# Two parts of a modulation vector summed on TensorE instead of VectorE, with a new order of steps, in a two-layer trunk on one core

## The chip, the core and the metric

The kernel runs on one core of one Trainium2 chip. The metric is the device time of one execution in microseconds (us), lower is better. The engines are named as the profile names them: PE is TensorE (its matmuls; PEld its weight loads, which run beside them), DVE is VectorE, ACT is ScalarE, POOL is GpSimd, SP is SyncE, which issues most DMAs.

## What is computed

A trunk of two layers over 512 positions with 1024 features each. Around every layer stands a modulation that depends on one vector c alone:

```python
cond = jax.nn.silu(c)
for l in range(DEPTH):                       # DEPTH = 2
    mod = cond @ ada_w[l] + ada_b[l]         # ada_w[l] is 1024 x 3072
    shift, scale, gate = jnp.split(mod, 3, axis=-1)
    h = rms_norm(x, norm_g[l]) * (1.0 + scale[:, None, :]) + shift[:, None, :]
    ...                                      # layer 0: conv + RWKV-7 heads, layer 1: sparse attention
    x = x + gate * mixed
```

The change touches `cond @ ada_w[l]`: a vector of 1024 times a matrix. Shift and scale of layer 0 are computed at the kernel's start, and gate of layer 1 near its end (both of these already on PE). What stays, gate of layer 0, shift of layer 1 and scale of layer 1, is 3 x 1024 numbers, in six parts of 512: the later modulation, M0 to M5.

Layer 0 has two halves that share one projection: a convolution of width 31 followed by a layer norm and two gates, and 16 RWKV-7 heads, done in eight pairs (a pair is called a head below, 0 to 7), each a recurrence over 8 chunks of 64 positions. Both go through one output projection. Layer 1 is attention over 16 heads with an indexer that keeps 128 keys for each query.

## The kernel before

**Layout and precision.** Features lie on the 128 partitions, the 512 positions along the free dimension. All dense products split both operands into a high and a low half and take three products per 128 x 128 weight tile (L369). For that, ACT writes a weight tile's high half (L355), and the low half is a subtraction on DVE or POOL (`low`, L337 to L339), chosen by step: steps named in the table `LOWV` use DVE.

**What sets the order.** The table `ORDER` lists layer 0 as steps: D (dense k, r, v of a head), P (prep), O (operands of the recurrence), G (gate), V (a conv block), A (the conv branch's gate), S (a triangular solve: 31 pairs of steps on DVE, L585 to L591, and DMA round trips), T (its second half on PE: 32x32 matmuls, L611 to L626), C (the chain over 8 chunks, L628 to L674), N (norm of a head, with a transpose `pyT` at L689), M0 to M5 (the later modulation), ln (layer norm statistics), Y and Z (the two halves' results), E (a1: output projection of 7 of the heads plus the conv branch's first part, `zo8qN`), W and F (a2: the rest of the output projection, `zo0qN`). A scheduler emits the steps in this order into the five engines' queues, shifted by priorities: the table `PRIO` gives an offset for a step or a tile ("0S" the solve's tiles, "pvar" the sums of the layer norm's variance, "1K" layer 1's keys, and so on). Each engine then runs its own queue in order and waits for others by semaphores. `START` and `ORDER1` do the same for the first steps and for layer 1.

**The chain, one chunk.** Two products `px` from the state SV; a copy to X on ACT (L649); two more `px`; two `py` and, after a copy of SV on ACT (L662), `py<-SV,BKn`, which carries the state on; then DVE adds it to the decayed state: `SV<-py,sw` (L671). The next chunk's first product waits for that addition. Each float32 matmul stands twice in the trace's counts (x4 there is 2 in the code).

**A part of the later modulation, `ada_col(n)`, L726 to L745.** Eight tiles `at` of 128 x 512 are loaded on ACT's DMA queue (L732); DVE multiplies the first by a column of `cond` (L734) and adds the other seven in turn into `ac` (L736: 128 x 512 each); then four one-column matmuls with a column of ones sum over the partitions (`pmc`, L740, a 128 x 128 weight load each), and DVE adds the bias into `modc` (L742). From the step `late` on, `at` and `ac` come from a pool with 4 buffers that `yb`, `xa`, `xl` and `sq` (tiles of Y, E and F) share.

**Layer norm.** ln sums the squares of eight blocks `yc` on POOL (`vs`, L866); four one-column matmuls `pvar` (L870), a root taken over DVE and POOL (`rs`, L209 and L210), a copy (L200) and a transpose-broadcast `pbc` (L203) follow; the Z steps wait for the result.

Of the kernel before, what the change touches and what calls it, by code (L numbers as in the profile page):

```python
# [10 lines left out]
F32 = mybir.dt.float32  # L11
F32R = mybir.dt.float32r
I32 = mybir.dt.int32
AF = mybir.ActivationFunctionType
# [4 lines left out]
P = 128  # L19
D = 1024  # L20
S = 512
KT = D // P
# [14 lines left out]


ORDER = """
D0 lora V0 P0 D1 D2 O0 G0 P1 P2 O1 S0.1 T0 C0 V1 T1 C1 M0 rot D3 O2 P3 M1 O3 N0 G1 D4 G2 S2.3 V3 A6 T2 C2 P4 V4 D5  # L40
T3 V2 O4 N2 P5 A7 C3 G3 O5 S4.5 V6 N1 G4 T4 C4 V5 N3 M4 T5 V7 C5 D6 A2 P6 G5 O6 D7 P7 O7 A1 S6 G7 T6 late G6 N4 A3
A0 Y3 A4 Y4 N5 S7 A5 ln M3 C6 Y0 Z7 T7 N6 Y1 C7 Z3 Y2 M2 Y5 Z6 Y6 Z0 E6 E3 Z1 E1 M5 E4 Z2 E2 E5 E0 N7 E7 Z5 Z4 W
F7.1 F5 F1 F7.0 F4 F0 F2 F3 F6.0 F6.1
"""


PRIO = {"conv": -1552, "0D": -465, "0N": 74, "1K": -464, "1w": -326, "1x": -48, "0S": 206, "0M": -31, "1y": -15, "0rot": 1, "0G": -123, "1m": -706, "0lora": 36, "0A": -118, "1I": 556, "0Y": -189, "0Z": 12, "pmean": 97, "0V": 5, "0late": 493, "pvar": -495, "pbn": -87, "1k": -9, "xs": 74}


LOWV = ('0A', '0D', '0E', '0F', '0G', '0N', '0V', '0Y', '0Z', '1e', '1ki', '1qi', '1v', '1y')  # L50


ACT0 = "XBrt"


START = """
x0 b0 a0 g1 g2 h0 g3 b1 h1 a1 b2 z0.3 z0.1 z0.0 x4 x5 a2 h3 a3 h2 x6 z0.2 h5 h4 x7 z2.2 z1.2 z1.1 z1.0 z2.3 z1.3 b3
z2.1 h6 z2.0 h7 z3.0 z3.2 z3.1 z3.3
"""


# [12 lines left out]
def trunk(ctx: ExitStack, tc: tile.TileContext, x, c, positions, ada_w, ada_b, norm_g, final_g,  # L74
# [3 lines left out]
    V, A, G, T, DQ = nc.vector, nc.scalar, nc.gpsimd, nc.tensor, nc.sync  # L78
# [5 lines left out]

    PR = PRIO

    def prio(key):
        return tc.high_priority(offset=PR[key]) if key in PR else nullcontext()
# [5 lines left out]
    cst = ctx.enter_context(tc.tile_pool(name="cst", bufs=1))  # L94
# [5 lines left out]
    def zps(name="z"):  # L100
        return ps.tile([P, 512], F32, tag="z", bufs=3, name=name)

    def tps(tag, bufs):
        return lambda shape, name: ps.tile(shape, F32, tag=tag, bufs=bufs, name=name)


    cps, pps, aps = tps("c", 2), tps("p", 2), tps("a", 1)


    ident = cst.tile([P, P], F32, name="ident")  # L110
# [27 lines left out]
    ones_col = ones_m[:, 0:1]  # L138
# [7 lines left out]
    for tb in range(TB):  # L146
        t = pa.tile([P, D], F32, tag="x", bufs=5, name="xt")
# [20 lines left out]
    nc.scalar.dma_start(prm3, bass.AP(tensor=conv_w.tensor, offset=conv_w.offset,  # L168
                                      ap=[[P, 124], [124 * P, 2], [1, P]]))

    cond = cst.tile([P, KT], F32, name="cond")
    tc_ = cst.tile([P, KT], F32, name="tc_")
    A.activation(tc_, cc, AF.Tanh, scale=0.5)
    V.scalar_tensor_tensor(out=cond, in0=tc_, scalar=1.0, in1=cc, op0=OP.add, op1=OP.mult)
# [4 lines left out]
    C0 = (C_LORA, C_K, C_R, C_V)  # L179
    at0, w0 = [[None, None] for _ in range(4)], []  # L180
    for w in "w0 00 w1 11 01 w2 10 21 20 31 w3 30".split():
        i, n = w[0], int(w[1])
# [63 lines left out]
    Z0 = [zps("z0") for _ in range(3)] + [cps([P, 512], "z0") for _ in range(4 - 3)]  # L246
# [67 lines left out]
    S0 = dict(a=lambda q: mod0(q, 0), b=lambda q: mod0(q, 1), x=lambda k: xn(k, "D"), g=lambda k: xn(k, "G"), h=h0, z=z0)  # L314
# [77 lines left out]
    def slab(tag, bufs, name, dt=F32):  # L392
        return pq.tile([P, 512], dt, tag=tag, bufs=bufs, name=name)
# [332 lines left out]
    def ada_col(n, slab):  # L726

        l, c0 = (0, 2 * D + n * 512) if n < 2 else (1, (n - 2) * 512)
        ac = slab("ac")
        for k in range(KT):  # L730
            t = slab("at")
            nc.scalar.dma_start(t, ada_v[l, :, k, c0:c0 + 512])  # L732
            if k == 0:
                V.tensor_scalar(ac, t, cond[:, 0:1], None, op0=OP.mult)  # L734
            else:
                V.scalar_tensor_tensor(out=ac, in0=t, scalar=cond[:, k:k + 1], in1=ac, op0=OP.mult, op1=OP.add)  # L736
        pm = aps([P, 4], "pmc")
        for j in range(4):
            with prio("pm"):
                T.matmul(pm[:, j:j + 1], lhsT=ac[:, j * P:(j + 1) * P], rhs=ones_col, start=True, stop=True)  # L740
        m_ = modc[:, n * 4:n * 4 + 4]
        V.tensor_tensor(out=m_, in0=pm, in1=ab(l, (2, 0, 1)[n // 2])[:, n % 2 * 4:n % 2 * 4 + 4], op=OP.add)  # L742
        if n >= 4:
            V.scalar_tensor_tensor(out=m_, in0=m_, scalar=1.0, in1=PT2[:, 56 + (n - 4) * 4:60 + (n - 4) * 4],
                                   op0=OP.add, op1=OP.mult)  # L745
# [245 lines left out]
    def ops(h):  # L991
# [3 lines left out]
        lora=lora, rot=rotary, D=dense_h, P=lambda h: hp_prep(h, D_[h]), O=ops, S=lambda *h: hp_solve(h),  # L995
        T=lambda h: hp_solve2(H[h]), C=lambda h: hp_chain(H[h]), G=lambda h: hp_gate(h, H[h]),
# [36 lines left out]
    for tb in range(TB):  # L1033
        t = asl("pen", 4, "pen")
# [274 lines left out]
```

## Time and profile before

| | us |
|---|---|
| three runs before | 1263.14, 1264.27, 1270.81 |
| median | 1264.27 |
| the profiled execution | 1265.15 |
| its span in the trace | 1263.3 |
| PE busy in the span | 1169.2 (93%) |
| DVE / ACT / POOL busy | 983.0 (78%) / 610.1 (48%) / 311.4 (25%) |
| mean granted clock of PE | 0.946 of full speed |

The profile is that of one execution. Busy shares are averages over stages; the granted clock is 1.00 where PE runs at its upper level and 0.50 at its lower, and a stretch between is a mix of both. The rows that the prediction uses stand in the section below.

### The profile page before, as it was taken

To read this page: it belongs to the slowest core of one execution; us is meant where nothing else is said; L and a number is where in the kernel's file an instruction comes from. 1 tells how busy PE (TensorE), PEld (TensorE's weight loads), DVE (VectorE), ACT (ScalarE), POOL (GpSimd) and SP (SyncE) were. 2 spreads that over 40 slices of the span, in tenths; PEclk is the share of its full clock that TensorE was granted. 3 is DMA by queue.
4 is the path that set the end of the run, shared out by engine and by line. 5 is a ranking of instruction groups with operands and counts; after the bars stand their busy time and mean duration, and the time that the engine had idled before them with its cause. 6 is when DMAs were issued, how large, how long until landed. Compare 5 with 4: busy or idle time off the path is not lost. (4 is left out here: it accounts for less than half of the span.)

```text
span 1263.3 us, 19449 instructions
## 1 busy us (share of the span) xinstructions
PE 1169.2 (93%) x6984; PEld 930.0 (74%) x6984; DVE 983.0 (78%) x2080; ACT 610.1 (48%) x1322; POOL 311.4 (25%) x344
## 2 busy tenths in 40 slices
PE   5999999999999999989689998899999999999997
PEld 2676677878776777766568787776777788888886
DVE  5759888669878998887876646679999899958732
ACT  4355454653355444445345334445453566636433
POOL 3113113210223111421232003424565110020042
PEclk8899998899979998999578999899999999999998
DMA  9623335323311323125555743643444422232122
GB/s 291 181 68 99 88 103 159 105 73 109 83 56 55 105 65 92 52 71 165 169 169 184 216 146 100 197 105 117 125 134 125 138 64 75 56 100 62 49 86 84
DMA packets 204007, 142.83 MB, mean 113 GB/s; under 512 B 33373, under 2 KB 176134, under 8 KB 203910
## 3 DMA queue, kind: packets, MB, share of 16 engines
q1 hardware_dynamic: 187616, 114.88, 31.6%
q10 hardware_dynamic: 16294, 26.70, 7.3%
q8 instruction: 55, 0.90, 0.3%
q14 instruction: 42, 0.34, 0.1%
HBM read 117.69 MB, written 17.83 MB: 107 GB/s over the span
## 5 line engine op out<-in xcount | busy, mean ns | idle before, releaser
L355 ACT ACTIVATE wh<-st 128x512 fp32r<-128x512 f32 (+2 forms) x256 | 148.7, 606 | 211.1 <-issue 34.6
L339 POOL TENSOR_TENSOR wl<-st,wh 128x512 fp32r<-128x512 f32 x82 | 115.0, 1416 | 306.1 <-ACT wh L355 298.8
L713 DVE SCALAR_TENSOR_TENSOR cacc<-u,PT,cacc 128x512 f32<-128x512 f32 x240 | 183.3, 782 | 1.5
L339 DVE TENSOR_TENSOR wl<-st,wh 128x512 fp32r<-128x512 f32 (+2 forms) x174 | 115.4, 674 | 44.9 <-ACT wh L355 44.7
L659 POOL TENSOR_TENSOR sw<-SV,W 64x128 f32<-64x128 f32 x56 | 59.1, 1059 | 130.0 <-DVE SV L671 118.9
L1186 ACT ACTIVATE lm<-lm,mx 128x512 f32<-128x512 f32 x64 | 46.1, 720 | 32.4 <-DVE mx L1185 32.3
L1194 ACT ACTIVATE pth<-pt 128x512 fp32r<-128x512 f32 x64 | 37.7, 593 | 35.4 <-PE pt L1192 28.5
L1183 DVE CUSTOM_DVE_ANT_0 lm<-pl,pen 128x512 f32<-128x512 f32 x64 | 43.3, 682 | 10.9 <-PE pl L1177 8.2
L1195 DVE TENSOR_TENSOR ptl<-pt,pth 128x512 fp32r<-128x512 f32 x64 | 43.5, 685 | 5.9 <-ACT pth L1194 5.8
L673 ACT ACTIVATE Y<-py 64x128 f32<-64x128 f32 x64 | 17.1, 267 | 55.9 <-DVE SV L671 48.1
L1122 DVE MATCH_REPLACE8 sc<-m,sc 128x512 f32<-128x512 f32 x64 | 42.8, 675 | 0.0
L1192 PE MATMUL pt<-ident,lm 128*128 128x128 f32 x256 | 39.1, 275 | 3.8 <-DVE lm L1188 2.3
L589 DVE TENSOR_TENSOR tmp<-TA,En 128x126 f32<-128x126 f32 (+37 forms) x155 | 40.5, 261 | 2.1
L1121 DVE MAX8 m<-sc 128x8 f32<-128x512 f32 x64 | 41.4, 681 | 0.0
L640 PEld LDWEIGHTS px<-SV,LTR 128*65 128x65 f32 x256 | 26.4, 158 | 20.1 <-DVE SV L671 13.5
L591 DVE TENSOR_TENSOR En<-En,tmp 128x126 f32<-128x126 f32 (+37 forms) x155 | 38.7, 250 | 2.2
L640 PEld LDWEIGHTS py<-SV,BKn 128*65 128x65 f32 x224 | 21.1, 155 | 25.4 <-ACT SV L662 22.9
L1192 PEld LDWEIGHTS pt<-ident,lm 128*128 128x128 f32 x256 | 29.3, 140 | 13.0 <-issue 8.6
L736 DVE SCALAR_TENSOR_TENSOR ac<-at,cond,ac 128x512 f32<-128x512 f32 x42 | 32.9, 783 | 7.5 <-DMA at<-in_ada_w 7.5
L640 PE MATMUL px<-SV,LTR 128*65 128x64 f32 x256 | 30.5, 249 | 8.1 <-DVE SV L671 7.4
L1208 PE MATMUL pO<-pth,vrh 128*128 128x256 f32 x128 | 37.1, 290 | 0.6 <-DVE gr L1212 0.6
L662 ACT ACTIVATE SV<-px 64x128 f32<-64x128 f32 x64 | 17.2, 269 | 41.8 <-PE px L640 26.6
(1262 smaller groups left out, 3775.9 us busy)
## 6 DMA issues: line engine op xcount, KB each, us to landing
st<-in_even_w_in SPq DMA_DIRECT2D x57, 512.0 KB, 4.1
st<-in_odd_w_in SPq DMA_DIRECT2D x38, 512.0 KB, 4.6
at<-in_ada_w ACTq DMA_DIRECT2D x48, 256.0 KB, 2.7
ast<-in_ada_w SPq DMA_DIRECT2D x8, 1024.0 KB, 10.7
st<-in_odd_w_out SPq DMA_DIRECT2D x16, 512.0 KB, 4.0
st<-in_even_w_out SPq DMA_DIRECT2D x9, 512.0 KB, 4.2
yc<-cv_d SPq DMA_DIRECT2D x16, 256.0 KB, 3.9
gt<-in_ada_w ACTq DMA_DIRECT2D x16, 256.0 KB, 3.8
```

What stands on the lines that cost most here:

```text
L339: (V if STEP[0] in LOWV else G).tensor_tensor(out=dst, in0=src, in1=hi.bitcast(F32), op=OP.subtract)
L355: A.activation(wh[c_], st[c_], AF.Copy)
L589: V.tensor_tensor(out=tv, in0=TA[:, j, j + 1:32, None].to_broadcast([P, n, m]), in1=E_[:, j:j + 1, :m].to_broadcast([P, n, m]), op=OP.mult)
L640: T.matmul(out[0:m, s_], lhsT=L[r_, o:o + m], rhs=rhs[r_], skip_group_check=True, **k_)
L659: G.tensor_tensor(out=f2(sw), in0=f2(SV[0:64, c_]), in1=wb, op=OP.mult)
L713: V.scalar_tensor_tensor(out=ac, in0=u[:, j:j + S], scalar=wcol(j), in1=ac, op0=OP.mult, op1=OP.add)
L1121: V.max(out=m8, in_=sc)
L1122: V.match_replace(out=sc, in_to_replace=m8, in_values=sc, imm_value=-3e38)
L1183: V.tensor_tensor_reduce(out=lm, in0=pl, in1=pen[tb], scale=1.0, scalar=-3e38, op0=OP.add, op1=OP.max, accum_out=mx[:, 0:1])
L1186: A.activation(lm, lm, AF.Exp, scale=ISQ, bias=mx[:, 1:2], accum_out=mx[:, 2:3])
L1192: T.transpose(pt[:, sb], lm[:, sb * P:(sb + 1) * P], ident)
L1195: V.tensor_tensor(out=ptl[:, :, s2], in0=pt, in1=pth[:, :, s2].bitcast(F32), op=OP.subtract)
```

## The change

Parts M3 and M5 (`MPE = "35"`) are summed by matmuls: for each of the eight `at` tiles PE adds `condw[:, k:k+65]` (transposed) times the tile to a 65 x 512 sum `p_row`; the vector c's tile is widened by 64 columns of zeros so that 65 columns can be taken from any k. Row 0 of the sum is the wanted one. ACT copies it into `ac`, and the four one-column matmuls pick row 0 with a column of the identity in place of the ones. M0, M1, M2 and M4 stay on DVE. Besides, `ORDER` (layer 0), `START`, `PRIO` and `LOWV` have new values. `ORDER1`'s text is the same.

```diff
-PRIO = {"conv": -1552, "0D": -465, "0N": 74, "1K": -464, "1w": -326, ..., "0S": 206, ..., "0lora": 36, ..., "0late": 493, "pvar": -495, ..., "xs": 74}
+PRIO = {"conv": -1552, "0D": -465, "0N": 76, "1K": -490, "1w": 8, ..., "0S": 289, ..., "0lora": 76, ..., "0late": 1067, "pvar": -430, ..., "pyT": 8, "pt": -23, ...}
...
-LOWV = ('0A', '0D', '0E', '0F', '0G', '0N', '0V', '0Y', '0Z', '1e', '1ki', '1qi', '1v', '1y')
+LOWV = ('0A', '0D', '0E', '0F', '0G', '0N', '0V', '0Y', '0Z', '1e', '1f', '1ki', '1v', '1y')
+MPE = "35"
...
-    cond = cst.tile([P, KT], F32, name="cond")
+    condw = cst.tile([P, KT + 64], F32, name="condw")
+    G.memset(condw[:, KT:], 0.0)
+    cond = condw[:, 0:KT]
...
         ac = slab("ac")
+        pe = str(n) in MPE
+        p_row = aps([65, 512], "p_row1") if pe else None
         for k in range(KT):
             t = slab("at")
             nc.scalar.dma_start(t, ada_v[l, :, k, c0:c0 + 512])
-            if k == 0:
+            if pe:
+                T.matmul(p_row, lhsT=condw[:, k:k + 65], rhs=t, start=k == 0, stop=k == KT - 1)
+            elif k == 0:
                 V.tensor_scalar(ac, t, cond[:, 0:1], None, op0=OP.mult)
             else:
                 V.scalar_tensor_tensor(out=ac, in0=t, scalar=cond[:, k:k + 1], in1=ac, op0=OP.mult, op1=OP.add)
+        r_ = slice(0, 65 if pe else P)
+        if pe:
+            A.activation(ac[0:65], p_row, AF.Copy)
         pm = aps([P, 4], "pmc")
         for j in range(4):
             with prio("pm"):
-                T.matmul(pm[:, j:j + 1], lhsT=ac[:, j * P:(j + 1) * P], rhs=ones_col, start=True, stop=True)
+                T.matmul(pm[:, j:j + 1], lhsT=ac[r_, j * P:(j + 1) * P], rhs=ident[r_, 0:1] if pe else ones_col,
+                         start=True, stop=True)
```

Counted over the whole program, PE gets 16 matmuls `p_row` more; DVE has 14 multiply-adds and 2 multiplications of 128 x 512 fewer; ACT has 2 copies of 65 x 512 more; POOL has one memset more and 8 low halves fewer, DVE 8 low halves more (16 of layer 1's output projection come to it, 8 of the indexer's queries leave it). DMAs are the same in number and size. The line numbers after are larger by 6 to 14.

The order moves at many places of layer 0. Three of them matter below.

The first is PE's queue in the chain of head 6 (C6), where M3 stands. `px` and `py` are the chain's products, `pvar` and `pbc` belong to the layer norm. Before, with the chain's first chunk in the first two rows:

```order
L640 MATMUL py<-SV,BKn 65x64 x2
L640 MATMUL py<-SV,Q 65x64 x2
L870 MATMUL pvar<-ones_m,vs 128x1 x4
L640 MATMUL px<-SV,LTR 65x64 x2
L640 MATMUL py<-SV,LTR 65x64 x2
L203 MATMUL pbc<-ident,vs 128x128 x4
L640 MATMUL px<-X_544,Q 65x64 x2
L640 MATMUL py<-SV,BKn 65x64 x2
L640 MATMUL py<-SV,Q 65x64 x2
L640 MATMUL px<-SV,LTR 65x64 x2
```

After, from the end of the chain's second chunk:

```order
L884 MATMUL pvar<-ones_m,vs 128x1 x4
L742 MATMUL p_row_5955<-at,condw 65x512
L209 MATMUL pbc<-ident,vs 128x128 x4
L646 MATMUL px<-SV,LTR 65x64 x2
L742 MATMUL p_row_5955<-at,condw 65x512
L646 MATMUL py<-SV,LTR 65x64
L742 MATMUL p_row_5955<-at,condw 65x512
L646 MATMUL px<-X_544,Q 65x64 x2
L646 MATMUL py<-SV,LTR 65x64
L742 MATMUL p_row_5955<-at,condw 65x512
L646 MATMUL py<-SV,BKn 65x64 x2
L646 MATMUL py<-SV,Q 65x64 x2
```

Two chunks of the chain now stand ahead of `pvar`, where one stood, and the eight `p_row` are laid between the products of the third and fourth chunk. The eight `p_row` of M5 stand in E, after head 7's chain, between the products of `zo8q2x` and `zo8q4x`.

The second is DVE's queue at the same place. `rs<-pvar` needs `pvar` from PE; `SV<-py,sw` carries the chain from one chunk to the next; `tmp` and `En` are the solve of head 7 (S7). Before:

```order
L848 SCALAR_TENSOR_TENSOR yc<-yc,mean 128x512
L589 TENSOR_TENSOR tmp<-TA,En 128x68
L209 TENSOR_SCALAR rs_5943<-pvar 128x4
L591 TENSOR_TENSOR En<-En,tmp 128x17x4
L671 TENSOR_TENSOR SV<-py,sw 64x128
L589 TENSOR_TENSOR tmp<-TA,En 128x64
L200 COPY vs<-rs_5943 128x512
L591 TENSOR_TENSOR En<-En,tmp 128x16x4
```

After:

```order
L677 TENSOR_TENSOR SV<-py,sw 64x128
L595 TENSOR_TENSOR tmp<-TA,En 128x72
L862 SCALAR_TENSOR_TENSOR yc<-yc,mean 128x512
L597 TENSOR_TENSOR En<-En,tmp 128x18x4
L595 TENSOR_TENSOR tmp<-TA,En 128x68
L597 TENSOR_TENSOR En<-En,tmp 128x17x4
L862 SCALAR_TENSOR_TENSOR yc<-yc,mean 128x512
L595 TENSOR_TENSOR tmp<-TA,En 128x64
L597 TENSOR_TENSOR En<-En,tmp 128x16x4
L595 TENSOR_TENSOR tmp<-TA,En 128x75
L597 TENSOR_TENSOR En<-En,tmp 128x15x5
L215 TENSOR_SCALAR rs_5891<-pvar 128x4
```

The chain's first addition stood behind `rs<-pvar` and now stands ahead of it, and S7's steps are further on when `rs` comes (width 15 x 5 where it was 18 x 4).

The third is PE's queue at the end of head 5's chain, where dense work of the conv gate (`za`) and of a conv block (`zv7x`) stands beside the operands of head 7 (`pm`, `pk`) and the transpose of a normed head (`pyT`). Before:

```order
L517 MATMUL pm<-LTR,BK 128x128 x8
L369 MATMUL za3x<-hlo,wh 128x512
L689 MATMUL pyT<-ident,Y 128x128 x4
L369 MATMUL za3x<-hhi,wl 128x512
L369 MATMUL za3x<-hhi,wh 128x512
L517 MATMUL pm<-LTR,BK 128x128 x8
L369 MATMUL za3x<-hlo,wh 128x512
L369 MATMUL za3x<-hhi,wl 128x512
L369 MATMUL zv7x<-hhi,wl 128x512
```

After:

```order
L550 MATMUL pk<-ident,BK 128x128 x4
L375 MATMUL zv7x<-hlo,wh 128x512
L550 MATMUL pk<-ident,BK 128x128 x4
L375 MATMUL zv7x<-hhi,wl 128x512
L375 MATMUL zv7x<-hhi,wh 128x512
L375 MATMUL za4x<-hhi,wh 128x512
L375 MATMUL za4x<-hlo,wh 128x512
L375 MATMUL za4x<-hhi,wl 128x512
L695 MATMUL pyT<-ident,Y 128x128 x4
L375 MATMUL za4x<-hhi,wh 128x512
```

`pyT` stood between two products of `za3x` and ahead of the second set of `pm`; it now stands behind both sets of `pm`, the `pk` and all of `zv7x`.

Elsewhere, told from the same comparison: beside the chains of heads 0 and 1, 14 products of `zv3x` and `zb1x` stand in the first two chunks where 6 stood; DVE's low halves of the weights for `za5x` stand ahead of the `yc` of ln, where they stood among them; T of head 7 stands right behind the last chunk of head 6's chain, where products of `zo8q3x` and `zo8q6x` stood between; at the start of layer 1 POOL has the two low halves of one weight (for `y30x`) next to each other where another operation stood between them; from there to the softmax of layer 1 PE's queue is nearly the same, and behind it some products change places.

## Rows read from the trace of the kernel before

**Rows 1.** Page, section 1: engine, busy us (share of the span), instructions.

```profile
PE 1169.2 (93%) x6984; PEld 930.0 (74%) x6984; DVE 983.0 (78%) x2080; ACT 610.1 (48%) x1322; POOL 311.4 (25%) x344
```

**Rows 2.** Windows (us): length, busy us (count) by engine, PEclk, DMA share, GB/s.

```profile
190.00:200.00 10.00, 8.24 (x47) 6.37 (x47) 7.35 (x16) 3.47 (x9) 5.70 (x3) 0.66 0.52 150
220.00:240.00 20.00, 20.00 (x169) 16.91 (x166) 13.63 (x24) 12.07 (x31) 4.10 (x5) 0.74 0.28 76
360.00:380.00 20.00, 19.72 (x156) 16.53 (x156) 12.86 (x23) 14.34 (x31) 3.83 (x3) 0.66 0.21 60
560.00:600.00 40.00, 34.92 (x170) 26.07 (x171) 29.87 (x84) 21.99 (x46) 7.09 (x10) 0.93 0.45 130
600.00:650.00 50.00, 38.25 (x277) 31.06 (x276) 40.68 (x110) 21.59 (x51) 14.80 (x13) 0.57 0.56 169
650.00:690.00 40.00, 36.43 (x319) 29.55 (x318) 25.61 (x48) 20.88 (x52) 8.85 (x7) 0.87 0.55 168
690.00:720.00 30.00, 26.87 (x135) 21.48 (x134) 23.98 (x42) 13.72 (x26) 4.40 (x2) 1.00 0.79 237
790.00:800.00 10.00, 6.73 (x33) 6.00 (x34) 6.66 (x6) 4.42 (x8) 6.93 (x5) 0.66 0.53 150
1000.00:1200.00 200.00, 196.66 (x1133) 165.09 (x1132) 171.31 (x442) 114.95 (x242) 22.29 (x16) 1.00 0.25 68
```

**Rows 3.** Timeline of PE, 20 to 50: start, length, operation [idle before].

```profile
25.68 6.49 PE L274 MATMUL p_row<-ast,cond 128*1 128x256 f32 x16 [2.06 <-DMA ast<-in_ada_w]
...
32.83 3.61 PE L274 MATMUL p_row<-ast,cond 128*1 128x256 f32 x16
```

**Rows 4.** Page, section 5: the multiply-adds of all six parts on DVE.

```profile
L736 DVE SCALAR_TENSOR_TENSOR ac<-at,cond,ac 128x512 f32<-128x512 f32 x42 | 32.9, 783 | 7.5 <-DMA at<-in_ada_w 7.5
```

**Rows 5.** Page, section 6: loads of the modulation tiles, KB, us to landing.

```profile
at<-in_ada_w ACTq DMA_DIRECT2D x48, 256.0 KB, 2.7
```

**Rows 6.** Timeline of PE, 600 to 660: head 6's chain, and head 7's T.

```profile
609.01 0.70 PE L640 MATMUL py<-SV,BKn 128*65 128x64 f32 x4 [0.71 <-ACT SV L662]
...
612.00 1.86 PE L870 MATMUL pvar<-ones_m,vs 128*128 128x1 f32 x8 [1.85 <-POOL vs L866]
614.54 0.67 PE L640 MATMUL px<-SV,LTR 128*65 128x64 f32 x4 [0.68 <-DVE tmp L589]
...
624.65 0.70 PE L640 MATMUL px<-SV,LTR 128*65 128x64 f32 x4 [1.91 <-DVE SV L671]
...
650.91 0.64 PE L611 MATMUL p<-ident,Q 32*32 32x32 f32 x16
```

**Rows 7.** Timeline of DVE, 604 to 640: the same stretch.

```profile
613.90 0.16 DVE L209 TENSOR_SCALAR rs<-pvar 128x4 f32<-128x4 f32 x1 [0.58 <-PE pvar L870]
...
614.12 0.28 DVE L671 TENSOR_TENSOR SV<-py,sw 64x128 f32<-64x128 f32 x1
...
616.61 0.47 DVE L734 TENSOR_SCALAR ac<-at,cond 128x512 f32<-128x512 f32 x1
...
621.68 0.75 DVE L736 SCALAR_TENSOR_TENSOR ac<-at,cond,ac 128x512 f32<-128x512 f32 x1 [0.98 <-DMA at<-in_ada_w]
...
629.59 0.89 DVE L736 SCALAR_TENSOR_TENSOR ac<-at,cond,ac 128x512 f32<-128x512 f32 x1
...
636.31 0.36 DVE L591 TENSOR_TENSOR En<-En,tmp 128x8 f32<-128x8 f32 x1
```

**Rows 8.** Timeline of ACT, 600 to 640: loads of M3 in its DMA queue.

```profile
617.54 0.84 ACTq L732 DMA_DIRECT2D at<-in_ada_w  x2
...
622.46 2.18 ACTq L732 DMA_DIRECT2D at<-in_ada_w  x3
```

**Rows 9.** Timeline of PE, 560 to 600: two of its idle times.

```profile
566.97 0.73 PE L689 MATMUL pyT<-ident,Y 128*128 128x128 f32 x4 [2.00 <-DVE Y L686]
...
597.12 0.50 PE L369 MATMUL za5x<-hhi,wl 128*128 128x512 f32 x1 [1.91 <-DVE wl L339]
```

**Rows 10.** Timeline of PE, 686 to 720: the idle time in a1.

```profile
701.44 0.66 PE L904 MATMUL pX<-ident,xl 128*128 128x128 f32 x4 [2.22 <-DMA xl<-in_x]
```

More of the change, by code (lines that the diff above doesn't have):

```diff
@@ L39 @@
 ORDER = """
[L40 to L43, printed above, removed]
-"""
-PRIO = {"conv": -1552, "0D": -465, "0N": 74, "1K": -464, "1w": -326, "1x": -48, "0S": 206, "0M": -31, "1y": -15, "0rot": 1, "0G": -123, "1m": -706, "0lora": 36, "0A": -118, "1I": 556, "0Y": -189, "0Z": 12, "pmean": 97, "0V": 5, "0late": 493, "pvar": -495, "pbn": -87, "1k": -9, "xs": 74}
-LOWV = ('0A', '0D', '0E', '0F', '0G', '0N', '0V', '0Y', '0Z', '1e', '1ki', '1qi', '1v', '1y')
+D0 lora P0 V0 D1 D2 O0 G0 P1 P2 O1 S0.1 T0 C0 V1 T1 C1 M0 rot D3 O2 P3 N0 O3 G1 D4 S2.3 G2 V3 A6 T2 C2 V4 D5 M1 P4
+V2 T3 N2 O4 A7 C3 N1 P5 G3 O5 S4.5 T4 V6 N3 C4 V5 T5 M4 V7 C5 G4 D6 A2 P6 O6 G5 D7 P7 O7 A1 S6 late G7 T6 N4 G6 A3
+S7 A4 Y3 A0 Y4 ln A5 N5 M3 C6 Z7 Y0 N6 Y1 T7 C7 Y2 M2 Y5 Z6 Y6 Z1 Z0 E3 E6 M5 E2 E4 E1 E0 N7 Z2 E7 Z5 Z3 E5 Z4 W F5
+F4 F7.0 F3 F7.1 F1 F0 F2 F6.0 F6.1
+"""
+PRIO = {"conv": -1552, "0D": -465, "0N": 76, "1K": -490, "1w": 8, "1x": -48, "0S": 289, "0M": -31, "1y": -15, "0rot": 1, "0G": -123, "1m": -713, "0lora": 76, "0A": -118, "1I": 602, "0Y": -189, "0Z": 24, "0V": 5, "0late": 1067, "pvar": -430, "pbn": -87, "1k": -9, "0W": -384, "1e": 6, "pyT": 8, "pt": -23, "pmean": 94}
+LOWV = ('0A', '0D', '0E', '0F', '0G', '0N', '0V', '0Y', '0Z', '1e', '1f', '1ki', '1v', '1y')
+MPE = "35"
 ACT0 = "XBrt"
 START = """
-x0 b0 a0 g1 g2 h0 g3 b1 h1 a1 b2 z0.3 z0.1 z0.0 x4 x5 a2 h3 a3 h2 x6 z0.2 h5 h4 x7 z2.2 z1.2 z1.1 z1.0 z2.3 z1.3 b3
-z2.1 h6 z2.0 h7 z3.0 z3.2 z3.1 z3.3
+b0 x0 a0 g1 g2 g3 h0 b1 h1 a1 b2 z0.3 z0.1 z0.2 z0.0 x4 x5 a2 a3 h3 h2 h4 h5 x6 x7 z2.2 z1.2 z1.0 z1.1 z2.3 z1.3 b3
+z2.1 z2.0 h7 h6 z3.0 z3.2 z3.3 z3.1
 """
```

## The prediction

> **What bounds the kernel now.** I read the page's first section first: PE is busy for 1169.2 of 1263.3 us and DVE for 983.0 [rows 1]. So PE bounds the kernel on average, and any matmul that is added costs its full time unless it falls into a time in which PE waits. Taking work off DVE gains only where PE waits for DVE. Next come the windows, one stage per line [rows 2]. The reader should look at two columns of each: PE's busy time against the window's length (the difference is idle) and PEclk. From 1000 to 1200 PE is busy 196.66 of 200 us at a clock of 1.00: nothing can be won there except by less work. The poor stretches are 600 to 650, the chain of head 6 (11.75 us idle and a clock of 0.57, which is nearly the lower level throughout), 790 to 800, the start of layer 1 (3.27 idle, 0.66), 190 to 200 (1.76 idle, 0.66), 560 to 600 (5.08 idle), and the solves at 220 and 360, where PE is busy but at 0.74 and 0.66. Third, the timelines of the engines in 600 to 650 show what the chain waits for, since the change is put there [rows 6 to 8]. The sum is made against the profiled execution's 1265.15 us, which is 0.88 above the median of 1264.27.
>
> **What is added and removed.** DVE loses 14 of the 42 multiply-adds at 783 ns, 10.96 us [rows 4], and 2 multiplications at 0.47 [rows 7], 0.94: 11.9 us in all, half of it in C6. PE gains 16 matmuls of 512 columns. The nearest row is the first modulation's `p_row`, float32 too, with one column of weights instead of 65: 16 entries, that is 8 matmuls of 256 columns, take 6.49 us in one place and 3.61 in another [rows 3], a ratio of 1.8, so I read these as PE's lower and upper level. With twice the columns, 8 matmuls cost 13.0 at the lower level and 7.2 at the upper. The 64 further columns of weights are loaded by PEld beside the matmuls; I take them as free, since PEld is idle for a quarter of the span [rows 1]. M3 lies in C6 at the lower level, M5 in E, where the clock is 1.00 [rows 2]: 13.0 + 7.2 = 20.2 us of PE work. ACT's two copies of 512 columns are hidden: ACT is busy 48% [rows 1], and nothing waits for `modc` until layer 1. So on bare work the change is a loss: PE is the bound, and 12 us are taken from an engine that is not.
>
> **C6 and E, 600 to 720.** In C6 the state addition of the first chunk starts at 614.12, directly behind `rs` at 613.90, although its product was issued at 609.01 and lasted 0.70: it stood in DVE's queue behind a step that waits for the layer norm's sums [rows 6, 7]. The next chunk's first product starts at 614.54. In the new order the addition stands ahead of `rs`, and could run at about 610, so 4 us come off the chain. At 624.65 the chain waits 1.91 us for DVE, which is then busy with M3's multiply-adds [rows 6, 7]; they are gone: 2 us. Against this stand 13.0 us of `p_row` between two chunks. Their tiles arrive slowly as it is: M3's multiplications run from 616.61 to 629.59, 13 us for eight tiles, once waiting for the load [rows 7], and the loads stand in ACT's queue until buffers come free [rows 8]. PE's idle time from 600 to 720 is 11.75 + 3.57 + 3.13 = 18.45 us [rows 2], but the `p_row` have fixed places in its queue and the idle time has others (2.22 of it waits for `xl` [rows 10]), so I let 8 us of the 20.2 fall into it, a bit under half. The net is 20.2 - 4 - 2 - 8 = +6. Behind C6, T of head 7 started at 650.91, 14 us after S7's last step on DVE at 636.31, the solve's way through memory [rows 6, 7]. With S7 further on in the new order T comes earlier; but the products of `zo8q3x` that stood ahead of it have to be done all the same, so I count nothing for it. Bounds: if only the 2.22 us of idle are used, +12; if moreover nothing comes off DVE's waits, +18; if the clock rises in C6, the 38.25 busy us at 0.57 would be up to 16 shorter, which turns +6 into -10.
>
> **The new order elsewhere.** Each term is bounded by the idle time and the half-speed time that its window shows [rows 2], where a time at clock f could be shorter by (1 - f) of the busy time.
> - 190 to 200, chain of head 0: 1.76 idle and 0.34 x 8.24 = 2.8 from the clock. With 14 dense products instead of 6 in the first two chunks most gaps are filled: -3, between 0 and -4.6.
> - Solves at 220 and 360: 5.2 + 6.8 = 12.0 from the clock, no idle time. The order around them changes little: -2, between -6 and +3 (fill that is used earlier is missing later).
> - 560 to 600: two waits of 2.00 and 1.91 us, one for the transpose `pyT` that comes ahead of DVE's norm, one for `za5x`'s low halves [rows 9]. The new order moves exactly these two, `pyT` behind some fifteen products and the low halves ahead: -4, between 0 and -5.1.
> - 790 to 800: 3.27 idle, 2.3 from the clock. Two low halves of one weight next to each other on POOL shorten the wait: -4, between 0 and -5.6.
> - Layer 1 behind that: the queue is 98% busy at full clock; the low halves that change engine go to engines with room (POOL 25% busy): 0, between -3 and +4.
>
> Sum: +6 - 3 - 2 - 4 - 4 = -7. From 1265.15 that is 1258.15, and 0.88 less for the median: **1257 us**. All bounds together reach from -34 to +25, which is not to be expected at once.
>
> **A rule on the clock.** C6 shows 0.57 while PE is busy for 77% of the window, with short products and waits between; 690 to 720 shows 1.00 at 90% [rows 2]. The Trainium skill, page "TensorE: Matmul & The Clock Gate", section "Part 1: The HAM clock gate", says that the throttled state is the default and that activity releases it; so added matmuls in C6 may pay for themselves, and this kernel's rows agree in kind. By the bare sum C6 and E cost +6, by the rule up to 16 less.
>
> **The rivals.**
> - *The clock rises in C6 and at the start of M3.* For it: 65 columns of 512 in every gap of two chunks are far denser work than the chain's 64-column products. Against it: the `pvar`, `pbc` and chain products ahead left it at 0.57, and behind M3 the chain is as thin as before for four chunks. Price: I take 12 of the 16 us: 1257 - 12 = 1245.
> - *The idle time only moves.* PE is at 93%, and waits filled in one place come back at the next one, as DVE is still 78% busy; then the terms outside C6 and E are 0, and +6 stays: 1264.27 + 6 = 1270, no measurable change. For it: two thirds of the terms rest on orders whose waits I can't time.
> - *PE's queue is held by the loads (the other side).* PE takes its queue in order, so a `p_row` whose tile has not landed holds the chain's products behind it; the tile waits for a buffer, which an earlier `p_row` frees; and the chain's copy of SV on ACT stands behind such a load in ACT's queue (such issues last 0.84 us for two and 2.18 for three now [rows 8]). A round costs 2.7 us to landing [rows 5] and 1.6 for a `p_row` (13.0 / 8). With about two buffers left for the tiles there are three to four rounds: C6 gets 13 us of waits on top, and M5 in E 4 x (2.7 + 0.9) = 14.4 us of which 7.2 are its work, 7 more. With none of the 8 us hidden as well this is 28 over my sum: about 1283. It decides if PE reaches the third `p_row` before its tile is there, that is if idle time in front of `p_row` goes above 2 us twice. Against it: the tiles' 13 us in C6 are the length of the `p_row` work at the lower level, so loads and work may run in step.
>   The Trainium skill, same page, section "Part 2: What happens when you issue a matmul", says that only weight loads are pulled ahead and matmuls stay in program order, which is what this rival needs; the rows neither show nor deny it, for PE's records are in order here too.
>
> **How the numbers follow.** The forecast 0.42, the clock rising 0.25, idle time that only moves 0.20, held by the loads 0.13. About 1% is what a measurement of this kernel can tell, so faster means below 1251.6 and slower above 1276.9. Faster: 0.21 from the second case, 0.11 from the forecast's lower part (the terms with -6 to -5 taken fully): 0.32. Slower: 0.10 from the loads, 0.02 from the moved idle time: 0.12. Same: 0.56. The range from 1243 to 1275 holds the forecast with its bounds, the moved idle time and most of the clock's case; outside are the loads' case (0.12) and 0.07 below. The forecast's own range is 1250 to 1265.
>
> **What would show it right or wrong.** In C6 the first state addition comes within 1 us of its product, and the chain's second chunk begins 4 us earlier relative to T6's end; the `p_row` of M3 take 1.6 us each (lower level) or 0.9 (the clock rose), with under 1 us of wait ahead of each. From 560 to 600 the waits for `pyT` and `za5x` are gone, and 790 to 800 shows over 8 us of PE busy time. PE's busy time rises by 10 to 20 us, or less if the clock rises; DVE's falls by 12. The prediction is wrong if a wait of over 2 us for a load stands ahead of a `p_row` more than once, if PEclk of C6 is above 0.75, or if the total moves while the windows named here don't.

## The result, and the profile after

The changed kernel takes 1271.49 us (median of 20 runs, 1264.76 to 1282.72) against 1264.82 us before (20 runs, 1257.03 to 1272.52). The ratio is 1.0061 with a 95% interval from 1.0041 to 1.0081: slower by 0.6%, 7.7 us, where the forecast was 7 us faster. The profiled execution took 1272.99 us, its span is 1271.2 us. The runs of one kernel spread by 1% and more, so below a kernel's time is given as a ratio with its interval, and stages are compared in the traces.

The page of the changed kernel, section 1, answers to [rows 1]:

```profile
PE 1169.7 (92%) x7016; PEld 924.9 (73%) x7016; DVE 971.6 (76%) x2072; ACT 610.3 (48%) x1324; POOL 303.4 (24%) x337
```

DVE's busy time fell by 11.4 us, where 11.9 was counted. PE's is the same, although it got sixteen sums: the mean granted clock of this execution is 0.959, that of the profiled execution before 0.946, so PE spent less of its time at the lower level. The windows answer to [rows 2], the same columns:

```profile
220.00:240.00 20.00, 19.03 (x183) 16.44 (x184) 16.49 (x30) 13.25 (x38) 6.67 (x7) 1.00 0.42 124
360.00:380.00 20.00, 19.06 (x140) 16.28 (x138) 14.99 (x26) 12.58 (x31) 4.93 (x4) 0.82 0.25 75
560.00:600.00 40.00, 33.70 (x191) 24.82 (x190) 31.10 (x96) 22.16 (x49) 4.26 (x10) 0.99 0.43 118
600.00:650.00 50.00, 37.05 (x262) 25.45 (x259) 35.13 (x96) 20.72 (x48) 17.92 (x15) 0.66 0.55 168
650.00:690.00 40.00, 34.98 (x316) 28.68 (x315) 25.56 (x49) 18.93 (x48) 8.90 (x7) 0.87 0.56 173
690.00:720.00 30.00, 27.84 (x113) 18.11 (x114) 15.78 (x31) 13.02 (x25) 1.64 (x1) 0.94 0.61 181
```

The clock rose in four of these six windows and fell in one, and the kernel is slower all the same. Idle time in the chain of head 6 did not fall: 12.95 us of 50, where it was 11.75. PE's timeline in that chain answers to [rows 6]:

```profile
599.43 1.03 PE L617 MATMUL p<-ident,Q 32*32 32x32 f32 x16 [4.07 <-DMA Q<-ed]
...
610.48 0.70 PE L646 MATMUL px<-SV,LTR 128*65 128x64 f32 x4 [0.37 <-DVE SV L677]
...
616.56 0.70 PE L646 MATMUL py<-SV,BKn 128*65 128x64 f32 x4 [4.32 <-ACT SV L668]
...
620.55 1.95 PE L742 MATMUL p_row<-at,condw 128*65 128x512 f32 x2
...
623.60 0.64 PE L646 MATMUL px<-SV,LTR 128*65 128x64 f32 x4
...
631.17 1.07 PE L742 MATMUL p_row<-at,condw 128*65 128x512 f32 x2 [0.31 <-DMA at<-in_ada_w]
...
633.25 1.07 PE L742 MATMUL p_row<-at,condw 128*65 128x512 f32 x2 [1.00 <-DMA at<-in_ada_w]
```

The second chunk starts at 610.48, 4 us earlier than before, as forecast. Its product `py<-SV,BKn` then waits 4.32 us: the gain is given back within the same chunk. The third chunk starts at 623.60, behind `pvar`, a first sum and `pbc`; in the kernel before it started 4.2 us earlier:

```profile
619.42 0.70 PE L640 MATMUL px<-SV,LTR 128*65 128x64 f32 x4 [0.45 <-DVE SV L671]
```

The first row above shows one more wait: T of head 6 now waits 4.07 us for its solve's results to come back through memory, where it did not wait before. What holds the second chunk is seen on three other engines. First ACT and POOL:

```profile
616.24 0.27 ACT L668 ACTIVATE SV<-px 64x128 f32<-64x128 f32 x1 [0.84 <-POOL sw L665]
```

```profile
605.96 9.89 POOL L880 TENSOR_TENSOR vs<-vs,yc 128x512 f32<-128x512 f32 x5 [16.35 <-issue]
615.82 0.39 POOL L665 TENSOR_TENSOR sw<-SV,W 64x128 f32<-64x128 f32 x1
```

ACT's copy overwrites SV and so waits for POOL's decay product `sw` of the same chunk, which stands behind five additions of the layer norm's squares. The seven additions one by one (shortest, median, longest in ns):

```profile
L880 POOL TENSOR_TENSOR vs<-vs,yc x7: 1257/1262/4168, 606.0 to 617.5; 128x512 f32<-128x512 f32 x7
```

The longest is the first, from 605.96: DVE runs eight instructions of 0.22 to 0.69 us beside it, at their usual lengths, and the addition takes 4.17 us where its median sister takes 1.26. Some 2.9 of the five additions' 9.89 us come from this. Later it is DVE that is slowed. Its rows show one solve step while POOL is idle and two while it adds, with the chain's addition between:

```profile
604.07 0.23 DVE L595 TENSOR_TENSOR tmp<-TA,En 128x66 f32<-128x66 f32 x1
...
610.14 0.28 DVE L677 TENSOR_TENSOR SV<-py,sw 64x128 f32<-64x128 f32 x1 [1.14 <-PE py L646]
610.35 1.24 DVE L595 TENSOR_TENSOR tmp<-TA,En 128x72 f32<-128x72 f32 x1
...
614.65 1.29 DVE L597 TENSOR_TENSOR En<-En,tmp 128x72 f32<-128x72 f32 x1
```

M5's sums stand in dense work, four of them in one row, 3.85 us for 8 entries, 0.96 us each:

```profile
694.43 3.85 PE L742 MATMUL p_row<-at,condw 128*65 128x512 f32 x8
```

**Where the time went, by stage.** The table is made from the timelines of PE of all the profiles: T3, T4, T6 are the starts of the second solve half of heads 3, 4 and 6 (first `p<-ident,Q`), y18x and y24x the first product of these names in layer 1. The numbers are the time between (us). "Order alone" and the others are the experiments below; "before, again" is a second profile of the kernel before.

| kernel | to T3 | T3 to T4 | T4 to T6 | T6 to y18x | y18x to y24x | to the end |
|---|---|---|---|---|---|---|
| before | 359.3 | 129.7 | 111.9 | 171.1 | 35.1 | 456.3 |
| before, again (e5) | 360.6 | 126.6 | 111.0 | 173.0 | 35.6 | 456.4 |
| sums alone, old order (e2) | 352.2 | 128.3 | 115.3 | 181.6 | 34.8 | 457.1 |
| order alone (e1) | 357.0 | 131.7 | 105.2 | 171.8 | 31.2 | 454.3 |
| M3 only (e3) | 356.4 | 134.5 | 107.8 | 176.9 | 30.7 | 453.6 |
| M5 only (e4) | 357.8 | 131.7 | 104.8 | 175.3 | 31.1 | 454.0 |
| changed | 354.0 | 134.2 | 111.2 | 184.0 | 30.7 | 457.1 |

The stages up to T3 can't be compared: the first and third kernel have the same order there and differ by 7 us. From T6 to y18x, with the chain of head 6, E and F, the sums cost 8.6 to 10.5 us in the old order and 12 in the new, and the order alone changes nothing; each of these is one execution. From y18x to y24x every kernel with the new order is 4 us faster.

The length of a stage alone does not tell why it is long. The windows view of the two stages in the middle has PE's records and busy time (idle is the rest of the length, all in us) and the granted clock:

| kernel | T4 to T6: records, idle, clock | T6 to y18x: busy, idle, clock |
|---|---|---|
| before | 799, 7.6, 0.91 | 151.3, 19.8, 0.85 |
| before, again (e5) | 800, 9.1, 0.94 | 150.1, 22.9, 0.86 |
| sums alone, old order (e2) | 799, 8.0, 0.88 | 161.5, 20.1, 0.87 |
| order alone (e1) | 779, 10.9, 0.98 | 148.5, 23.3, 0.85 |
| changed | 779, 9.8, 0.91 | 162.7, 21.3, 0.87 |
| squares on DVE (e9) | 780, 9.2, 0.98 | 156.8, 21.7, 0.79 |
| M3 behind the chain (e11) | 779, 9.9, 0.98 | 170.6, 29.0, 0.81 |
| old middle (e12) | 799, 7.9, 0.88 | 148.9, 20.1, 0.85 |

From T6 to y18x the changed kernel has PE busy 14.3 us longer than the order alone, and only 2 us less idle: the sums found hardly any idle time to fall into. From T4 to T6 the new order has no less idle time than the old. It has 20 records fewer there, which stand in earlier stages, and the stage is short in the executions with a high clock and long in those with a low one.

### The profile page after: what moved, and what is told of

Read it like the earlier page. It is cut to its first block, busy times and chain, and to the rows that moved or that the text cites. A ratio compares the mean times of both kernels' runs of the same rounds, so it can differ in the third digit from the quotient of the medians.

```text
span 1271.2 us, 19519 instructions
## 1 busy us (share of the span) xinstructions
PE 1169.7 (92%) x7016; PEld 924.9 (73%) x7016; DVE 971.6 (76%) x2072; ACT 610.3 (48%) x1324; POOL 303.4 (24%) x337
## 5 line engine op out<-in xcount | busy, mean ns | idle before, releaser
L345 POOL TENSOR_TENSOR wl<-st,wh 128x512 fp32r<-128x512 f32 x74 | 104.9, 1433 | 259.2 <-ACT wh L361 238.0
L677 DVE TENSOR_TENSOR SV<-py,sw 64x128 f32<-64x128 f32 x56 | 15.7, 280 | 37.7 <-PE py L646 37.6
L646 PE MATMUL py<-SV,BKn 128*65 128x64 f32 x224 | 26.1, 243 | 16.4 <-ACT SV L668 16.4
```

The costliest lines, as they stand in the source:

```text
L646: T.matmul(out[0:m, s_], lhsT=L[r_, o:o + m], rhs=rhs[r_], skip_group_check=True, **k_)
```

## The experiments

Theory A: PE is the bound, so the sums cost their full time there, and what leaves DVE is worth nothing. Theory B: the sums are hidden and the new order's waits are the loss. Theory C: the tiles' loads hold PE's queue. Others are named where they come up. After each edit the scheduler lays the steps near it anew; in the traces the queues of PE, DVE, ACT and POOL are the same as in the kernel compared with for e5 and e6 alone.

**The two halves of the change apart (e1, e2).** The edit of e1, in the changed kernel; e2 is the kernel before with its tables, the change's code for the sums and `MPE = "35"`:

```diff
-MPE = "35"
+MPE = ""
```

> The changed kernel's order and tables with all six parts on DVE (no sums on PE). Theory A, PE pays for the sums in full: the trace of the changed kernel has 14 us more of PE work outside idle time and lower clock than before, so without the sums the time falls by 10 to 14 us below the changed kernel's 1271.5, to 1257 to 1262, a ratio to before of 0.994 to 0.998. Theory B, the new order's waits in the chains are the loss (8 us more idle time) and the sums are mostly hidden: 1267 to 1271, ratio 1.002 to 1.005.

> The order and tables of before, with M3 and M5 summed on PE as in the change. Theory A: before plus 8 to 14 us, 1273 to 1279, ratio 1.006 to 1.011. Theory B: before plus at most 4 us, ratio 1.000 to 1.003.

The order alone has a ratio to before of 0.9929 (0.9896 to 0.9963), the sums alone 1.0073 (1.0043 to 1.0103). In us of the 1263 before these are -9 and +9. Theory A holds and B falls: the order is a gain, and taking the sums back from the changed kernel gains 1.0061 - 0.9929 = 1.3%, 17 us. That is more than either theory gave, with an interval of some 5 us either way; the work itself is 15.4 us at the upper level (16 x 0.96). In the old order the sums cost 9 us, between 5 and 13, so there a part of them may have found idle time.

**One part at a time (e3, e4).** `MPE = "3"` and `MPE = "5"`.

> The changed kernel with only M3 on PE, M5 on DVE. Theory A: M3's eight matmuls cost 7 us in the chain of head 6 but the clock there rises and gives 4 back, so 2 to 5 us above the order alone. Theory C, PE's queue is held by the tiles' loads: M3 alone costs 8 us or more, with waits of over 1 us ahead of several of its matmuls. Theory B: within 2 us of the order alone.

> The changed kernel with only M5 on PE, M3 on DVE. Theory A: M5 stands between dense products at full clock, nothing hides it, so 6 to 9 us above the order alone. Theory C: more, 10 us or over, as it waits for loads too. Theory B: within 2 us of the order alone.

Ratios 0.9991 (0.9966 to 1.0016) and 0.9984 (0.9951 to 1.0017): 7.8 and 6.9 us above the order alone. Eight sums are 7.7 us of work, so each part costs about that, whether it stands in a chain with 13 us of idle time or in dense work. These differences have intervals of some 5 us either way; taken from the other side, leaving M3's sums off the changed kernel gains 9.7 us (e4 against it) and M5's 8.8 (e3). M3 was not shown to be cheaper, as I had expected from a rising clock. C falls for M5; M3's 7.8 is at its bound, but its waits are not: in the changed kernel all waits at the sums' line are these.

```profile
L742 PEld LDWEIGHTS p_row<-at,condw x32: 133/138/233, 620.5 to 700.7; 128*65 128x65 f32 x32
L742 PE MATMUL p_row<-at,condw x32: 592/593/1095, 620.6 to 701.1; 128*65 128x512 f32 x32
...
its engine sat idle before it (us, times) until:
...
  DMA at<-in_ada_w: 5.3, 7
```

These are PE's and PEld's instructions of line L742 (shortest, median, longest in ns) and what they waited for. PE's own are two of the seven, the 0.31 and 1.00 us above; the other five are PEld's, whose loads run ahead beside the matmuls. In their own profiles M3 has one wait of PE for a tile, 0.69 us (e3), and M5 one of 0.25 (e4). Theory C needed a wait at every round.

**The 64 zero columns (e6).** One column of weights instead of 65, with sum, copy and one-column products of one row accordingly (not shown); the order on every engine is unchanged.

```diff
-                T.matmul(p_row, lhsT=condw[:, k:k + 65], rhs=t, start=k == 0, stop=k == KT - 1)
+                T.matmul(p_row, lhsT=condw[:, k:k + 1], rhs=t, start=k == 0, stop=k == KT - 1)
```

> The changed kernel with one column of weights in the sums instead of 65 (no zero columns), the same order on every engine. Theory A, PE pays by streamed columns: the same time as the changed kernel, ratio to before 1.004 to 1.008, and each of the sums takes as long. Theory D, the 65 columns keep the clock up: the clock in the chain of head 6 stays near 0.57 and the time is 4 to 8 us above the changed kernel, ratio 1.009 to 1.013.

The ratio is 1.0055 (1.0029 to 1.0082), as the changed kernel's. The same view of its `p_row`:

```profile
L742 PEld LDWEIGHTS p_row<-at,condw x32: 79/82/85, 616.4 to 700.9; 128*1 128x1 f32 x32
L742 PE MATMUL p_row<-at,condw x32: 590/592/1057, 616.4 to 701.4; 128*1 128x512 f32 x32
```

The matmul takes 592 ns with 1 column and 593 with 65. The weight load is 56 ns shorter, beside the matmuls. The Trainium skill, page "TensorE: Matmul & The Clock Gate", section "Step-by-step: what each phase is for", says that a matmul's time goes by its number of streamed columns; the two rows, with 512 each, agree. The zero columns neither cost nor bring anything that these runs can tell.

**The price of DVE's share and of PE's (e7, e8).** e7 is the order alone without the 14 multiply-adds of M3 and M5, e8 the changed kernel without 14 of the 16 sums; both leave out part of the modulation. The edits:

```diff
-            else:
+            elif n not in (3, 5):
                 V.scalar_tensor_tensor(out=ac, in0=t, scalar=cond[:, k:k + 1], in1=ac, op0=OP.mult, op1=OP.add)
```

```diff
-            if pe:
-                T.matmul(p_row, lhsT=condw[:, k:k + 65], rhs=t, start=k == 0, stop=k == KT - 1)
+            if pe and k:
+                pass
+            elif pe:
+                T.matmul(p_row, lhsT=condw[:, k:k + 65], rhs=t, start=True, stop=True)
```

> The order alone (all on DVE), leaving out the 14 multiply-adds of M3 and M5 on DVE (their tiles are loaded and, but for the first, not used). It prices what the change takes off DVE. Theory A, DVE's work there is covered: 0 to 3 us below the order alone, ratio to before 0.990 to 0.993. The forecast's view, DVE's work in the chain of head 6 is waited for: 4 to 8 us below it, ratio 0.986 to 0.990.

> The changed kernel, leaving out 14 of the 16 sums on PE (only the first tile of M3 and of M5 is multiplied; all loads, both copies and the one-column products stay). It prices what the change puts on PE. Theory A: 12 to 16 us below the changed kernel, near the order alone, ratio to before 0.990 to 0.996. Theory C, the wait for the tiles and the copies' places are the price: 8 us or less below it, ratio 0.998 or more.

e7 has 0.9955 (0.9928 to 0.9981): not below the order alone at all. So leaving out 11 us of DVE's work, half of it in a chain in which PE waits for DVE, gains nothing that shows; the two intervals leave room for 2 us at most, which is what the forecast gave it. e8 has 0.9956 (0.9924 to 0.9988), 13 us below the changed kernel for 14 sums. The two agree: without either engine's sums the kernel takes what it takes with DVE's.

**The clock, drawn anew (e5).** The kernel before, unchanged.

> The kernel before, unchanged, for a second profile. If the clock at one place is a property of the order, PE's lower-level time comes within 3 us of the first profile's in each stretch (220 to 240 at 0.74, 360 to 380 at 0.66, 600 to 650 at 0.57). If it is drawn anew in every execution, stretches differ by 0.15 or more in clock while idle time agrees within 3 us, and then no term of the forecast that was read from the clock of one execution can be trusted.

```profile
220.00:240.00 20.00, 19.93 (x238) 16.65 (x236) 17.21 (x31) 14.75 (x37) 4.16 (x6) 1.00 0.41 122
360.00:380.00 20.00, 19.69 (x188) 16.05 (x188) 15.35 (x27) 16.22 (x35) 4.53 (x5) 0.83 0.22 61
600.00:650.00 50.00, 36.66 (x283) 29.76 (x280) 39.86 (x101) 21.80 (x52) 16.23 (x13) 0.66 0.55 167
```

These windows of e5 answer to [rows 2]: 1.00 where it was 0.74, 0.83 for 0.66, 0.66 for 0.57. The span is 1263.2 us, before it was 1263.3. So the same queues ran at a clearly higher clock in three poor stretches and ended at the same time: PE was busy 10 us less (1159.0 for 1169.2) and idle 10 us more. In the chain of head 6 the idle time is 13.34 us for 11.75, so part of the lower level there lies within waits for other engines; from T6 to the T of head 7 the chain still took 48.3 us at a clock of 0.65 where it had taken 50.1 at 0.58.

One pair of executions is a poor sample, though. Of the kernel before, 93 more executions stand beside the experiments, with a mean granted clock between 0.941 and 0.962 and a time between 1273 and 1253 us. The third of them with the lowest clock averages 0.947 and 1267.3 us, the third with the highest 0.959 and 1259.7; a straight line through all gives 6.7 us (5.6 to 7.9) less for 0.01 more. So where in a kernel the clock is low is drawn anew in every execution, but how much of it an execution gets does go with its time. And the new order got more: 0.961 on average in the order alone and in the changed kernel, 0.953 in the kernel before. By that line, an estimate, 5 of the order's 9 us go with its higher clock. What in the order raises it no run shows.

**The squares on DVE (e9).** Theory E: POOL's five additions are what took the chain's gain.

```diff
-                G.tensor_tensor(out=vs, in0=vs, in1=t, op=OP.add)
+                V.tensor_tensor(out=vs, in0=vs, in1=t, op=OP.add)
```

> The order alone (all sums on DVE), with the seven additions of the layer norm's squares (vs) on DVE instead of POOL. Theory E: in the chain of head 6 the new order won nothing because POOL's decay product (sw) of the second chunk stands behind five vs additions, and because DVE's short solve steps take 1.2 to 1.3 us instead of 0.22 while POOL adds. Then the second chunk's wait of 2 to 4 us goes, no solve step there is over 0.5 us, the stretch from head 6's second solve half to layer 1's first dense product is 3 to 6 us shorter than the order alone's 171.8 us, and the ratio to before is 0.988 to 0.991. Rival: the layer norm's sums take DVE's time instead and the chain waits for those: the same stretch within 2 us, ratio 0.992 to 0.996.

The ratio is 1.0004 (0.9972 to 1.0036), 9 us worse than the order alone, and T6 to y18x takes 178.5 us. PE and DVE in the chain of head 6:

```profile
614.87 1.87 PE L884 MATMUL pvar<-ones_m,vs 128*128 128x1 f32 x8 [5.40 <-DVE vs L880]
```

```profile
610.23 0.23 DVE L597 TENSOR_TENSOR En<-En,tmp 128x72 f32<-128x72 f32 x1
```

The waits that the theory named are gone (a solve step of 128 x 72 takes 0.23 us where it took 1.29), and one of 5.40 us for the same sums, now on DVE, is in their place; here `pvar` stands behind the first chunk, not the second. All in all the stage's idle time is not longer than in the order alone (21.7 us for 23.3). PE is busy 8.3 us longer over the same 993 records, at a clock of 0.79 for 0.85, and over all its executions e9 was granted 0.952, the order alone 0.961: what e9 lost goes with the lower clock, and why that is lower stays open. That the five additions hold the second chunk in the changed kernel is in its rows; that moving them to DVE would gain is wrong.

**Layer 1's start (e10).** The order alone with one priority as before (one entry of the line `PRIO`):

```diff
-"1w": 8,
+"1w": -326,
```

> The order alone with layer 1's weight priority (1w) as before, so that POOL's two low halves at the start of layer 1 are apart again. The forecast's term of 4 us there: the stretch from layer 1's first dense product to the third is 34 to 36 us again instead of 31.2, and the ratio to before is 0.995 to 0.998. Rival, the gain there comes from something else: 30 to 32 us and no change of the total.

The ratio is 0.9979 (0.9945 to 1.0012), and y18x to y24x takes 34.9 us for 31.2. The waits of PE in y30x, first in e10, then in the order alone:

```profile
788.21 0.39 PE L375 MATMUL y30x<-h1hi,wl 128*128 128x256 f32 x1 [0.90 <-POOL wl L345]
791.02 0.58 PE L375 MATMUL y30x<-h1hi,wh 128*128 128x256 f32 x1 [1.35 <-ACT wh L361]
793.99 0.58 PE L375 MATMUL y30x<-h1hi,wl 128*128 128x256 f32 x1 [1.66 <-POOL wl L345]
```

```profile
784.43 0.38 PE L375 MATMUL y30x<-h1hi,wl 128*128 128x256 f32 x1 [0.89 <-POOL wl L345]
787.12 0.39 PE L375 MATMUL y30x<-h1hi,wl 128*128 128x256 f32 x1 [0.85 <-POOL wl L345]
```

The stage's 3.7 us are shown to come from this priority, which holds for all of layer 1's weights. Of the 2.2 us by which these waits differ, POOL's low halves have 0.8 and ACT's high half 1.35. The ratio moved by 0.5%, but the two intervals overlap.

**M3 behind the chain (e11).** In the changed kernel's order (a stretch of its third line):

```diff
-N5 M3 C6 Z7 Y0 N6 Y1 T7 C7 Y2
+N5 C6 Z7 Y0 N6 Y1 T7 C7 M3 Y2
```

> The changed kernel with step M3 moved behind head 7's chain, so that its eight sums on PE stand in dense work and none between the products of head 6's chain. Theory A, PE pays in full wherever they stand: the changed kernel's time within 3 us, ratio to before 1.003 to 1.008. Rival, the stall of the chain is part of the price: 4 to 7 us less than the changed kernel, ratio 1.000 to 1.003.

Both expectations fell: 1.0178 (1.0119 to 1.0237), 15 us slower than the changed kernel. T6 to y18x takes 199.6 us. From its timeline of PE:

```profile
614.28 0.70 PE L646 MATMUL py<-SV,BKn 128*65 128x64 f32 x4 [2.24 <-ACT SV L668]
...
649.49 1.97 PE L742 MATMUL p_row<-at,condw 128*65 128x512 f32 x2
...
653.23 3.67 PE L742 MATMUL p_row<-at,condw 128*65 128x512 f32 x4
```

The chain of head 6 keeps its waits, the first sums run in the next one at the lower level (1.8 to 2.0 us each), and PE waits for tiles in five places, 2.7 us in all, where it was 1.3 in two. So "in full wherever they stand" is too simple: the place decides, and C6 was a better one than this. In the profile the stage is 15.6 us longer over the same 1024 records of PE: 7.7 us more idle time (29.0 for 21.3), and 7.9 us more busy time at a clock of 0.81 for 0.87. Which steps bring the idle time and the lower clock I can't name.

**The middle of layer 0 (e12).** The order alone, with the steps from T3 to C5 in the sequence of before (the lines joined).

```diff
-V4 D5 M1 P4 V2 T3 N2 O4 A7 C3 N1 P5 G3 O5 S4.5 T4 V6 N3 C4 V5 T5 M4 V7 C5 G4 D6
+M1 P4 V4 D5 T3 V2 O4 N2 P5 A7 C3 G3 O5 S4.5 V6 N1 G4 T4 C4 V5 N3 M4 T5 V7 C5 D6
```

> The order alone (all sums on DVE), with the middle of layer 0 (the steps from head 3's second solve half to head 5's chain) in the sequence of before. In the profiles the stretch from head 3's second solve half to head 4's took 126.6 to 129.7 us in the order of before and 131.6 to 134.5 in the new one. Theory F, the new sequence in that stretch costs 2 to 5 us: it comes back to 126 to 130, the later stretches keep the new order's gains, and the ratio to before is 0.988 to 0.991 (the order alone had 0.993). Rival, the difference is only where work is counted, and what is done earlier there is missing later: the stretch from head 4's to head 6's second solve half gets longer by as much, ratio 0.991 to 0.996.

T3 to T4 comes back to 128.5 us, and T4 to T6 rises to 115.2 from 105.2: the ratio is 0.9934 (0.9906 to 0.9962), the order alone's. The total is what the rival said, and theory F's 0.991 lies just inside the interval. Of the 10 us, a part is work that a sequence does earlier in one stage and lacks in the next: 20 of PE's records come back to this one. Another part goes with the clock, 0.88 for 0.98 in these two executions; how the two share it is not told apart. The wait at T6's start is gone as well: each of the ten profiles with the new middle has 3.2 to 5.2 us there, and none of the four with the old one has any. The order alone and e12 are the fastest whole kernels of this study, faster than both of the case.

## Why the prediction was wrong

The range (1243 to 1275) held the time, and "within 1%" was the likeliest outcome, but the sign was wrong: -7 for +7.7. Two parts of the sum failed by about 8 us each. The sums were to cost 20.2 - 2 - 8 = 10 us net, and cost 17 (the changed kernel against e1; 13 by e8). The new order was to bring 4 in C6 and 13 elsewhere, and brought 9. Point by point:

- **The price of a sum was about right.** I had 0.9 us at the upper level and 1.6 at the lower; they took 0.96 and, for a few, 1.95. That the 65 columns are free is shown (e6). The rows of all sixteen add up to 19.1 us (10.3 for M3, 8.8 for M5), close to the 20.2, though most of M3's ran at the upper level.
- **"I let 8 us of the 20.2 fall into idle time" failed.** This step decides the sign. From T6 to y18x PE is busy 14.3 us longer than in the order alone and idle only 2 us less. Each part costs its 7 to 8 us (e3, e4), both 13 to 17. Why the idle time doesn't take them is argued, not shown: the chain's idle times are steps that wait for each other, so a sum between two products of the chain delays the next step.
- **"2 us for DVE's multiply-adds" was not found.** Leaving them out gains nothing (e7), within some 2 us.
- **"4 us for the addition ahead of `rs`" failed one step later.** The addition came 4 us earlier, as forecast; then ACT's copy waited for `sw` on POOL, behind five additions. I had followed DVE's and PE's queues and not POOL's, although the `sw` of the very next chunk stands there. In the order alone the second chunk waits too, 3.08 us for DVE's addition and 2.24 for the copy, and the stage is unchanged (171.8 for 171.1 and 173.0).
- **The terms for 190 to 200 and the solves (-5 together) could not be read from one profile.** Where the clock is low is not a property of the kernel (e5). The gaps at 190 to 200 did close, from 1.76 to 0.43 us, but from T of head 0 to T of head 1, the stage around them, the new order takes 34.7 to 36.0 us and the old one took 35.0 to 36.9. Yet the new order did get a higher clock on average over its executions, worth some 5 us by the estimate under e5. I had not forecast that; where it agrees with my -5, that is luck.
- **560 to 600 (-4) failed: the waits moved.** The wait for `pyT` is 0.51 us for 2.00 and that for `za5x` is gone, as forecast. In their place T6's first product waits 4.07 us for its solve's way through memory, and the window's idle time is 6.30 us for 5.08. I had followed the two waits and not what the next step of the same queue waits for. That T4 to T6 is shorter in most kernels with the new order is moved work and a higher clock.
- **790 to 800 (-4): right**, 4 us, from the priority that I had in mind (e10); POOL's two low halves are the smaller part of it.
- For the order outside C6 and E I had -13, and the order alone gave -9 (interval -13 to -5) with C6 in it. Of these, 4 are shown to be layer 1's start; the other 5 are about what its higher clock is worth by the estimate. What raises the clock is open.

Of the rivals, "the idle time only moves" (1270) came nearest, by luck in the number: its +6 for C6 and E and nothing elsewhere were +17 and -9. Its mechanism is seen in one place, at T6. "Held by the loads" fell: two waits of 0.31 and 1.00 us in C6; its price was also added up wrongly, 1257 + 28 is 1285 and not 1283. "The clock rises" came true in the row (0.66 for 0.57), but without the sums the kernel before shows 0.66 too (e5) and the order alone 0.63. The rule of the Trainium skill, page "TensorE: Matmul & The Clock Gate", section "Part 1: The HAM clock gate", that activity releases the throttle, was weighed at up to 16 us there; these rows do not show a gain that the sums brought.

## What to carry to other kernels

Where one engine is over 90% busy, do not credit idle time to work that is moved onto it: here sixteen sums cost nearly their length, half of them in a stretch in which that engine idles a quarter of the time, and relieving an engine that was 78% busy gained nothing that could be measured. Both can be priced on their own by leaving the work out, as long as one looks at what the scheduler then moves. When a step is moved ahead in one queue, follow its next three waits through the queues of all engines, since the gain lasts only up to the next instruction that stands behind something long. Before a term is read from the clock of a stretch, take more profiles of the same kernel, and compare two kernels' clocks over all their executions. And take a stage's length apart into idle time, work and clock before it is explained.

## What the runs showed of the hardware

DVE's short additions and multiplications of the solve (two inputs, 128 x 60 to 128 x 76) take 0.22 us alone and 1.24 to 1.54 while POOL adds 128 x 512 tiles, and 0.23 at the same place when POOL does not (e9). It goes the other way too: where eight DVE instructions kept their lengths, POOL's addition took 4.17 us for 1.26. The Trainium skill, page "SBUF — State Buffer", section "Who interferes with whom", says that a DVE instruction with two inputs in SBUF contends with GpSimd's reads; these rows agree. The second surprise is that two executions with the same span (1263.2 and 1263.3 us) can differ by 0.26 in the granted clock of a 20 us stretch, while over 93 executions of one kernel 0.01 of the mean granted clock goes with 6.7 us.
